# Loading the first stage's pieces of w_in from Pool's queue, and leaving adaLN's columns alone in SP's

## The chip, the cores and the metric

One core of one Trainium2 chip. The metric is the device time of one execution in microseconds; the median of three runs stands for a kernel. An execution with the hardware profiler gives the trace that is read here.

## What is computed

One conditioned layer on a sequence of 256 tokens with 2048 features, all in float32. The input is normalised, scaled and shifted by a conditioning vector (adaLN), projected to four parts of 4096 columns, gated and convolved, projected back, and added to the input through a gate; a last normalisation follows. Cut to what matters:

```python
h = rmsnorm(x, norm_g)
mod = jnp.einsum('bd,df->bf', jax.nn.silu(c), ada_w) + ada_b   # 2048 -> 3 * 2048
shift, scale, gate = jnp.split(mod, 3, axis=-1)
h = h * (1.0 + scale) + shift
proj = jnp.einsum('bsd,de->bse', h, sc_w_in)                   # 2048 -> 4 * 4096
b_gate, c_gate, v, g = jnp.split(proj, 4, axis=-1)
u = causal_depthwise_conv(c_gate * v, sc_conv_w)
y = b_gate * u * jax.nn.silu(g)
out = rmsnorm(x + gate * jnp.einsum('bse,ed->bsd', y, sc_w_out), final_g)
```

## The kernel before

**Products.** Features lie on the partitions: `hT` holds the 2048 features of the tokens as 16 blocks `k` of 128 x 256. Each float32 operand is split into a high part (float32r) and a low part (what is left), and a product takes three matmuls: high by high, weight's high by tokens' low, weight's low by tokens' high (`product`, line 495). For a piece of weights that was loaded into a tile `raw`, ACT copies the high part (`hi`, line 354) and DVE subtracts to get the low part (`lo`, line 359); then TensorE may use the piece. `raw`, `hi` and `lo` have three tiles of 1 MB each, used in turn; a piece of 512 KB takes half of one. A `raw` tile is free again when DVE has made the low parts of what is in it.

**First stage.** The first half of the columns of w_in, in 16 groups of 512 columns: four chunks `ch`, each with four quarters `q`. The products can't wait for all of adaLN, since its columns of ada_w come in during the stage: eight groups of two feature blocks. So each group of 512 columns is worked in several passes over `k` (`part`, line 520), each over the blocks that are ready by then, 56 passes in all, and the sums of a pass stay in `acc` between passes (`keep`, line 512: copied by ACT or added by DVE; line 528 seeds a bank with an earlier sum). `plan` (line 52) fixes the order of the passes and of the column loads from a table of estimated costs. The first thirteen passes take the two feature blocks that are ready at the start, 512 KB of w_in each (the first of them has its own load, line 198); the fourteenth pass takes four blocks, 1 MB, and is the first to need the second group of columns.

**adaLN's columns.** `ada_piece` (line 454) loads a piece of 512 KB in two loads (shift and scale, line 464) into one of four tiles `at`, and DVE adds it up, weighted with silu(c) (`gv`, lines 476 and 478). When a group's eight pieces are in, `ada_done` (line 480) turns the sums on TensorE (`tp_g`, line 485) and reduces them on DVE (`gs`, 486; `mod`, 324); ACT makes the high parts of two token blocks (`hT`, 328), DVE the low parts (332 and 335).

**The gate's columns.** From the last third of the stage on, `gate_piece` loads the gate's columns of ada_w (`at_g`, line 612) into the same four tiles, DVE adds them up (`gacc`, 619 and 621; two buffers, shared with `gv`), and Pool adds the sums over the partitions in seven rounds per quarter of the gate: two copies from SBUF to SBUF by DMAs that Pool issues (625, 626) and an addition (627), then one with the bias (629).

**Second and last stages.** The other half of w_in's columns in pieces of 1 MB (line 665), and then w_out (line 720), with the residual and the last normalisation.

**Queues and order.** Before the change every load of weights stands in SP's queue, in the order of the program; a load waits there until its tile is free, and all loads behind it wait too. Pool issues only the gate's copies, ACT three small loads at the start. Within each engine the framework's scheduler sets the order of the instructions from an estimated timeline, with priorities from the program (`later`, line 189). So a load that is estimated to come earlier also moves instructions on DVE, ACT and TensorE. Each engine works its instructions strictly in that order.

Of the kernel before, what the change touches and what calls it, by code (L numbers as in the profile page):

```python
# [117 lines left out]
def short_conv_layer(ctx: ExitStack, tc: tile.TileContext, x, c, norm_g, ada_w, ada_b, w_in, conv_w, w_out, final_g, out):  # L118
    nc = tc.nc
# [58 lines left out]
    @contextmanager  # L178
    def behind(last):

        traced = nc.cur_bb.bb.instructions
        n = len(traced)
        yield
        for ins in list(traced[n:]):
            if ins.engine in last:
                tc.add_manual_dep(ins, last[ins.engine], after, reason="behind")
# [111 lines left out]
    def tokens(k, part):  # L298
        return (hT[:, k] if k < KB else hT2[:, k - KB])[:, part * T : (part + 1) * T]
# [14 lines left out]
    def keep_x(j, tp):  # L314
        for i in range(CT):
            k = j * CT + i
            nc.scalar.activation(xs[j][:, i], tp[:, i], AF.Copy, scale=gT[:, k : k + 1])
# [34 lines left out]
    def split_hi(raw, n, hi=None):  # L352
        hi = hi_tile() if hi is None else hi
        nc.scalar.copy(hi[:, :n], raw[:, :n])  # L354
        return hi

    def split_lo(raw, n, hi, lo_tag="lo", lo=None):
        lo = lo_tile(lo_tag) if lo is None else lo
        last_low[0] = nc.vector.tensor_tensor(  # L359
            out=lo[:, :n], in0=raw[:, :n], in1=hi[:, :n].bitcast(F32), op=ALU.subtract  # L360
        )
        return hi, lo
# [4 lines left out]
    def places(n):  # L367

        if n <= HALF and other_half[0]:
            tiles, other_half[0] = other_half[0], None  # L370
            return [b[:, HALF:SLOT] for b in tiles]
        tiles = raw_tile("raw_s"), hi_tile(), lo_tile()
        other_half[0] = tiles if n <= HALF else None
        return tiles
# [76 lines left out]
    acc = {}  # L451
# [49 lines left out]
    def chunk_products(bank, hi, lo, o0, k, k0, k1, seed=False, late=False):  # L501


        begins = k == k0 and not seed
        terms = [(m, i) for i in (0, 2, 1) for m in range(CT)] if late else [(m, i) for m in range(CT) for i in range(3)]
        for m, i in terms:
            o = slice(o0 + m * P, o0 + (m + 1) * P)
            product(bank[:, m, :], hi[:, o], lo[:, o], k, i, begins and i == 0, m % 2 == 0, k == k1 - 1 and (m, i) == terms[-1])
# [3 lines left out]
    def keep(ch, q, k0, bank, seed=False):  # L512
        if k0 == 0 or seed:
            if k0 == 0:
                acc[ch, q] = slot([P, CT, T], f"acc{ch}{q}")
            nc.scalar.copy(acc[ch, q], bank)  # L516
        else:
            nc.vector.tensor_tensor(out=acc[ch, q], in0=bank, in1=acc[ch, q], op=ALU.add)

    def part(ch, q, k0, k1, seed):  # L520


        col = q * E + ch * CT * P
        step = SLOT // (CT * P)
        first = k0
        bank = psum.tile([P, CT, T], F32, tag="mm", name="mm_s")
        if seed:
            nc.scalar.copy(bank, acc[ch, q])  # L528
        if pieces0:
            for k in range(NK0):  # L530
                chunk_products(bank, *pieces0[k], 0, k, k0, k1, late=True)
            pieces0.clear()
            k0 = NK0
        for s0 in range(k0, k1, step):
            sk = min(step, k1 - s0)
            n = sk * CT * P
            raw, hi, lo = places(n)
            nc.sync.dma_start(
                raw[:, :n].rearrange("p (k f) -> p k f", k=sk),
                w_in[0, s0 * P : (s0 + sk) * P, col : col + CT * P].rearrange("(k p) f -> p k f", p=P),  # L540
            )
            with behind(ended if len(acc) < 3 else {}):
                split_lo(raw, n, split_hi(raw, n, hi), lo=lo)
            for i in range(sk):
                chunk_products(bank, hi, lo, i * CT * P, s0 + i, k0, k1, seed)
        if len(acc) == 1:
            with behind(ended):
                keep_x(3, tp_3)
        keep(ch, q, first, bank, seed)
# [18 lines left out]
    for kind, *step in plan():  # L568
        if kind == "ada":
            ada_piece(*step)  # L570
        else:
            ch, k1 = step[0], step[3]
            part(*step)
            if step[2] == 0 and len(acc) in LATER:
                with tc.issue_after(last_mm[0].ins), behind(ended):
                    if len(acc) == LATER[0]:
                        rows2 = rows_tile("rows2")
                        nc.sync.dma_start(rows2[:, :], conv_w.rearrange("w (k p) -> (w k) p", p=P))
                    else:
                        turn(rows2, 0, 96, cw)  # L580
            whole[ch] += k1 == KT
            if k1 == KT and whole[ch] == 4:
                mixed(ch)
# [354 lines left out]
```

## Time and profile before

| | us |
|---|---|
| median of 3 runs | 904.29 (903.64 to 904.36) |
| the profiled execution | 904.01 |
| its span, first to last instruction | 902.2 |
| TensorE busy (matmuls) | 887.1, 98% of the span |
| DVE, ACT, Pool busy | 676.2, 484.5, 88.0 |
| moved by DMA | 235.01 MB, 260 GB/s on the mean |
| of it from SP's queue and from Pool's | 226.56 MB and 7.34 MB |
| granted TensorE clock | 0.998 |

The profile page gives each engine's busy time, 40 slices of the span with a digit for the busy share in tenths, and the chain of work that ended last, followed back from the end. Further views of the trace list instructions in order of time (start, duration, engine, line, output <- inputs, and in brackets the idle time before with what ended it), who waited for whom, and the busy time of each engine in a stretch. In a row of the latter stand, after the stretch and its length, busy time and number of instructions of PE (matmuls), PEld (weight loads), DVE, ACT and POOL, then the granted clock, the DMA share and GB/s. "SPq" is the issuing of a DMA by SP; how long it takes to land is told apart.

### The profile page before, as it was taken

What the parts mean: (1) busy time and instruction counts of PE and PEld (TensorE: products, weight loads), DVE (VectorE), ACT (ScalarE), POOL (GpSimd) and SP (SyncE); (2) the same over time, 40 slices, a digit from 0 to 9 for tenths busy, and PEclk for the clock granted to TensorE, in tenths of its full rate; (3) what the DMA queues carried; (4) which work ended last, traced back from release to release, by engine and by line L of the source; (5) the groups of instructions that cost most, each with busy time, mean ns of one, the idle gap of its engine ahead of it and who ended that gap; (6) DMA issues with size and microseconds to landing.
All of it is one profiled execution on the core that took longest, in us unless ns stands there. A gap on an engine that the chain in (4) does not pass through costs nothing.

```text
span 902.2 us, 16405 instructions
## 1 busy us (share of the span) xinstructions
PE 887.1 (98%) x6997; PEld 850.1 (94%) x6997; DVE 676.2 (75%) x665; ACT 484.5 (54%) x429; POOL 88.0 (10%) x95
## 2 busy tenths in 40 slices
PE   7999999999999999999999999999999999999996
PEld 4899999999999999999999999999999988888885
DVE  5889989888888866765966677565555578879896
ACT  6767866665548766644433434444434445444443
POOL 0000000000000034024224203420000000000000
PEclk9999999999999999999999999999999999999999
DMA  9999999999998587688887788776666476674662
GB/s 309 367 369 369 362 313 353 351 370 354 350 328 289 162 277 245 194 257 243 282 242 241 249 283 259 232 221 199 198 188 188 141 288 224 191 275 132 197 231 94
DMA packets 159595, 235.01 MB, mean 260 GB/s; under 512 B 6805, under 2 KB 105285, under 8 KB 159137
## 3 DMA queue, kind: packets, MB, share of 16 engines
q1 hardware_dynamic: 156384, 226.56, 76.9%
q0 software_dynamic: 3008, 7.34, 2.9%
q8 instruction: 55, 0.90, 0.4%
q14 instruction: 20, 0.16, 0.0%
q10 hardware_dynamic: 128, 0.04, 0.0%
HBM read 224.49 MB, written 2.10 MB: 251 GB/s over the span
## 4 chain that ended last, share of the span: by engine, by line
PE 92%; DMA 4%; ACT 1%; SPq 1%; DVE 1%; issue 1%; ACTq 0%
PE mm_b L495 39%; PE mm_s L495 36%; PE mm_w L731 7%; PE mm_o L731 6%; PE mm L731 4%; DMA at<-in_ada_w_dram 2%; DMA raw_s<-in_sc_w_in_dram 1%; SPq L231 1%; ACT hi L354 1%; DMA raw_o<-in_sc_w_out_dram 1%; DMA x<-in_x_dram 1%; PE tp_g L485 0%; ACT mm_s L528 0%; ACT acc L516 0%; DVE lo L762 0%
## 5 line engine op out<-in xcount | busy, mean ns | idle before, releaser
L495 PE MATMUL mm_s<-hT,hi 128*128 128x256 f32 x2048 | 350.2, 277 | 1.7 <-ACT hT L328 1.0
L495 PE MATMUL mm_b<-hT,hi 128*128 128x256 f32 x2048 | 348.2, 276 | 0.0
L495 PEld LDWEIGHTS mm_s<-hT,hi 128*128 128x128 f32 x2048 | 308.4, 188 | 2.3 <-ACT hT L328 1.2
L495 PEld LDWEIGHTS mm_b<-hT,hi 128*128 128x128 f32 x2048 | 308.4, 188 | 0.0
L495 PE MATMUL mm_b<-hT,lo 128*128 128x256 f32 x1024 | 282.7, 276 | 0.0
L495 PE MATMUL mm_s<-hT,lo 128*128 128x256 f32 x1024 | 282.0, 277 | 0.1
L359 DVE TENSOR_TENSOR lo<-raw,hi 128x2048 fp32r<-128x2048 f32 (+1 forms) x66 | 151.9, 2302 | 99.6 <-ACT hi L354 99.4
L354 ACT CAST hi<-raw 128x2048 fp32r<-128x2048 f32 (+1 forms) x66 | 123.7, 1874 | 191.3 <-PE mm_b L495 152.4
L495 PEld LDWEIGHTS mm_b<-hT,lo 128*128 128x128 f32 x1024 | 192.3, 188 | 0.0
L495 PEld LDWEIGHTS mm_s<-hT,lo 128*128 128x128 f32 x1024 | 191.7, 188 | 0.3 <-DVE lo L359 0.3
L359 DVE TENSOR_TENSOR lo<-raw_s,hi 128x2048 fp32r<-128x2048 f32 (+1 forms) x80 | 149.8, 1877 | 40.5 <-ACT hi L354 39.9
L354 ACT CAST hi<-raw_s 128x2048 fp32r<-128x2048 f32 (+1 forms) x80 | 124.0, 1557 | 57.2 <-PE mm_s L495 51.2
L478 DVE SCALAR_TENSOR_TENSOR gv<-at,silu_c,gv 128x512 f32<-128x512 f32 x105 | 78.7, 749 | 3.6 <-DMA at<-in_ada_w_dram 1.9
L516 ACT COPY acc<-mm_s 128x1024 f32<-128x1024 f32 x54 | 54.7, 1014 | 42.1 <-PE mm_s L495 42.0
L359 DVE TENSOR_TENSOR lo<-raw_o,hi 128x2048 fp32r<-128x2048 f32 x22 | 50.4, 2291 | 23.4 <-ACT hi L354 23.4
L354 ACT CAST hi<-raw_o 128x2048 fp32r<-128x2048 f32 x22 | 42.0, 1908 | 46.2 <-PE mm_w L731 12.0
L627 POOL TENSOR_TENSOR gacc<-gacc,z 128x512 f32<-128x512 f32 x28 | 48.3, 1726 | 109.0 <-DMA z<-gacc 109.0
L731 PE MATMUL mm_w<-hi,y 128*128 128x512 f32 x184 | 58.8, 389 | 0.0
L731 PE MATMUL mm_o<-hi,y 128*128 128x512 f32 x176 | 55.3, 389 | 0.0
L621 DVE SCALAR_TENSOR_TENSOR gacc<-at_g,silu_c,gacc 128x512 f32<-128x512 f32 x60 | 46.9, 782 | 6.0 <-DMA at_g<-in_ada_w_dram 4.8
L625 POOL DMA_DIRECT2D z<-gacc x28 | 15.7, 560 | 348.7 <-DVE acc L562 284.7
L731 PEld LDWEIGHTS mm_w<-hi,y 128*128 128x128 f32 x184 | 34.5, 188 | 7.1
(153 smaller groups left out, 685.9 us busy)
## 6 DMA issues: line engine op xcount, KB each, us to landing
raw<-in_sc_w_in_dram SPq DMA_DIRECT2D x64, 1024.0 KB, 5.9
raw_s<-in_sc_w_in_dram SPq DMA_DIRECT2D x47, 1024.0 KB, 7.8
raw_o<-in_sc_w_out_dram SPq DMA_DIRECT2D x32, 1024.0 KB, 5.2
at<-in_ada_w_dram SPq DMA_DIRECT2D x114, 256.0 KB, 8.0
raw_s<-in_sc_w_in_dram SPq DMA_DIRECT2D x33, 512.0 KB, 7.1
at_g<-in_ada_w_dram SPq DMA_DIRECT2D x32, 512.0 KB, 7.9
at<-in_ada_w_dram SPq DMA_DIRECT2D x6, 512.0 KB, 9.4
x<-in_x_dram SPq DMA_DIRECT2D x4, 512.0 KB, 6.2
```

The costliest lines, as they stand in the source:

```text
L231: nc.sync.dma_start(at[:, :, s, :], adas[:, j : j + kk, s, 0 : NK0 * P])
L354: nc.scalar.copy(hi[:, :n], raw[:, :n])
L359: last_low[0] = nc.vector.tensor_tensor(out=lo[:, :n], in0=raw[:, :n], in1=hi[:, :n].bitcast(F32), op=ALU.subtract)
L478: nc.vector.scalar_tensor_tensor(out=gv, in0=at4[:, i], scalar=c_k, in1=gv, op0=ALU.mult, op1=ALU.add)
L495: mm = last_mm[0] = nc.tensor.matmul(dst, w, h[k], start=begins and left, stop=ends, skip_group_check=True)
L516: nc.scalar.copy(acc[ch, q], bank)
L621: nc.vector.scalar_tensor_tensor(out=ga, in0=at3[:, i, :], scalar=s, in1=ga, op0=ALU.mult, op1=ALU.add)
L625: nc.gpsimd.dma_start(turned[0 : P - away], ga[away:P])
L627: nc.gpsimd.tensor_tensor(out=ga, in0=ga, in1=turned, op=ALU.add)
L731: nc.tensor.matmul(dst, y[a], b, start=opens and i == 0, stop=ends and i == 2, skip_group_check=True)
```

## The change

In `part`, pieces of w_in go to Pool's queue once five groups of columns have been begun. `acc` gets an entry at the end of a group's first pass, so `len(acc) < 5` holds for the first five passes. The first has its weights from line 198; the second to the fifth load one piece each. So of the 80 loads of line 538, the first four stay with SP and the other 76 are issued by Pool.

```diff
             sk = min(step, k1 - s0)
             n = sk * CT * P
             raw, hi, lo = places(n)
-            nc.sync.dma_start(
+            queue = nc.sync if len(acc) < 5 else nc.gpsimd
+            queue.dma_start(
                 raw[:, :n].rearrange("p (k f) -> p k f", k=sk),
                 w_in[0, s0 * P : (s0 + sk) * P, col : col + CT * P].rearrange("(k p) f -> p k f", p=P),
             )
```

From line 538 on, line numbers of the changed kernel are one higher. On SP, from the fourth piece on, the rows before are these (`raw_s` is a piece of w_in, 128x2x512 being 512 KB and 128x4x512 1 MB; `at` is half a piece of adaLN's columns):

```order
L538 DMA raw_s<-in_sc_w_in_dram 128x2x512
L464 DMA at<-in_ada_w_dram 128x2x256 x4
L578 DMA rows_621<-in_sc_conv_w_dram 96x128
L538 DMA raw_s<-in_sc_w_in_dram 128x2x512 x4
L464 DMA at<-in_ada_w_dram 128x2x256 x4
L538 DMA raw_s<-in_sc_w_in_dram 128x2x512 x2
L464 DMA at<-in_ada_w_dram 128x2x256 x4
```

In the changed kernel the same place of SP reads:

```order
L539 DMA raw_s<-in_sc_w_in_dram 128x2x512
L464 DMA at<-in_ada_w_dram 128x2x256 x4
L579 DMA rows_621<-in_sc_conv_w_dram 96x128
L464 DMA at<-in_ada_w_dram 128x2x256 x104
L613 DMA at_g<-in_ada_w_dram 128x2x512 x20
L666 DMA raw<-in_sc_w_in_dram 128x8x256 x6
```

All of adaLN's remaining columns and the first 20 loads of the gate's now follow each other, held only by their own four tiles. The pieces stand on Pool, behind its one instruction for the tokens of the start and ahead of the gate's copies:

```order
L433 TENSOR_TENSOR hT<-xs_169,hT 128x256
L539 DMA raw_s<-in_sc_w_in_dram 128x2x512 x8
L539 DMA raw_s<-in_sc_w_in_dram 128x4x512 x3
L539 DMA raw_s<-in_sc_w_in_dram 128x2x512 x5
L539 DMA raw_s<-in_sc_w_in_dram 128x4x512 x6
```

DVE up to the ninth piece, before. The row of four low parts is that of the fifth to eighth pieces:

```order
L359 TENSOR_TENSOR lo<-raw_s,hi 128x1024
L478 SCALAR_TENSOR_TENSOR gv<-at,silu_c,gv 128x512 x4
L359 TENSOR_TENSOR lo<-raw_s,hi 128x1024 x4
L478 SCALAR_TENSOR_TENSOR gv<-at,silu_c,gv 128x512 x4
L359 TENSOR_TENSOR lo<-raw_s,hi 128x1024 x2
```

And in the changed kernel:

```order
L359 TENSOR_TENSOR lo<-raw_s,hi 128x1024
L478 SCALAR_TENSOR_TENSOR gv<-at,silu_c,gv 128x512 x4
L359 TENSOR_TENSOR lo<-raw_s,hi 128x1024 x2
L478 SCALAR_TENSOR_TENSOR gv<-at,silu_c,gv 128x512
L359 TENSOR_TENSOR lo<-raw_s,hi 128x1024
L478 SCALAR_TENSOR_TENSOR gv<-at,silu_c,gv 128x512 x2
```

Four sums of columns still stand ahead of the fifth piece's low part; behind it, sums are spread between the low parts, earlier than before. DVE about the thirteenth piece (the first `lo` of 128x2048), before, from the low parts of the eleventh and twelfth on:

```order
L359 TENSOR_TENSOR lo<-raw_s,hi 128x1024 x2
L486 TENSOR_REDUCE gs<-tp_g 128x4
L324 TENSOR_TENSOR mod<-gs,vec 128x2x2
L476 TENSOR_SCALAR gv<-at,silu_c 128x512
L478 SCALAR_TENSOR_TENSOR gv<-at,silu_c,gv 128x512
L359 TENSOR_TENSOR lo<-raw_s,hi 128x2048
L478 SCALAR_TENSOR_TENSOR gv<-at,silu_c,gv 128x512
L332 TENSOR_SCALAR xs_169<-xs_169,mod 128x256 x2
L478 SCALAR_TENSOR_TENSOR gv<-at,silu_c,gv 128x512
L335 TENSOR_TENSOR hT<-xs_169,hT 128x256 x2
```

In the changed kernel, from the low part of the twelfth piece on:

```order
L359 TENSOR_TENSOR lo<-raw_s,hi 128x1024
L478 SCALAR_TENSOR_TENSOR gv<-at,silu_c,gv 128x512
L486 TENSOR_REDUCE gs<-tp_g 128x4
L324 TENSOR_TENSOR mod<-gs,vec 128x2x2
L332 TENSOR_SCALAR xs_169<-xs_169,mod 128x256
L335 TENSOR_TENSOR hT<-xs_169,hT 128x256
L332 TENSOR_SCALAR xs_169<-xs_169,mod 128x256
L478 SCALAR_TENSOR_TENSOR gv<-at,silu_c,gv 128x512
L335 TENSOR_TENSOR hT<-xs_169,hT 128x256
L478 SCALAR_TENSOR_TENSOR gv<-at,silu_c,gv 128x512
L359 TENSOR_TENSOR lo<-raw_s,hi 128x2048
```

The two token blocks' low parts have moved ahead of the thirteenth piece's low part, and so have two sums of columns. On ACT the two casts of the same token blocks (line 328) stand behind that piece's high part before and ahead of it in the changed kernel.

## The prediction

> **What bounds the kernel now.** I read the page first, then busy time by stretch, then who waits for whom on TensorE, then SP, DVE and ACT in order of time where TensorE is least covered. The head, the slices and the chain:
>
> ```profile
> span 902.2 us, 16405 instructions
> PE 887.1 (98%) x6997; PEld 850.1 (94%) x6997; DVE 676.2 (75%) x665; ACT 484.5 (54%) x429; POOL 88.0 (10%) x95
> PE   7999999999999999999999999999999999999996
> DMA  9999999999998587688887788776666476674662
> PE 92%; DMA 4%; ACT 1%; SPq 1%; DVE 1%; issue 1%; ACTq 0%
> ```
>
> TensorE is busy 887.1 of 902.2 us and is 92% of the chain, so whatever delays it in the first stage stays in the total: the stages behind it have no idle time to give back. The DMA engines stand at 9 in the first twelve slices (270 us): there TensorE and the DMA engines are both full. Busy time by stretch says how full:
>
> ```profile
> 30.00:40.00 10.00, 9.36 (x84) 9.16 (x82) 8.19 (x11) 7.40 (x10) 0.00 (x0) 1.00 1.07 367
> 40.00:50.00 10.00, 10.00 (x88) 10.00 (x89) 8.96 (x10) 7.71 (x8) 0.00 (x0) 1.00 1.07 361
> 60.00:70.00 10.00, 10.00 (x91) 10.00 (x90) 9.93 (x14) 6.66 (x7) 0.00 (x0) 1.00 1.07 370
> 90.00:100.00 10.00, 9.91 (x87) 9.72 (x87) 9.75 (x13) 9.97 (x11) 0.00 (x0) 1.00 1.07 364
> 150.00:200.00 50.00, 50.00 (x443) 50.00 (x442) 43.88 (x50) 31.57 (x27) 0.00 (x0) 1.00 1.04 354
> ```
>
> A full 10 us holds 91 matmuls, 0.11 us each. 84, 88 and 87 are a loss of 7 + 3 + 4 matmuls, **1.5 us**: all that a better order of loads could win between 30 and 100 us. DMA runs at about 367 GB/s there, DVE up to 9.93 of 10.
>
> **The change, part by part.** It adds and drops no instruction: 76 loads of w_in leave SP's queue for Pool's, and the scheduler, which sees other arrival times, sets DVE's, ACT's and TensorE's rows in another order. I count pieces (loads of line 538) from one. The first four stay on SP.
>
> *A, the fifth piece, about 39 us.* The rows of SP, Pool, DVE, the landing of the four column loads issued from 24.91 on, and the piece of the chain that follows:
>
> ```profile
> 24.91 3.76 SPq L464 DMA_DIRECT2D at<-in_ada_w_dram  x4
> 27.72 0.96 SPq L464 DMA_DIRECT2D at<-in_ada_w_dram  x1
> 30.83 3.18 SPq L538 DMA_DIRECT2D raw_s<-in_sc_w_in_dram  x4
> DMA to landing us min/median/max: 8.2/8.3/8.7
> 26.02 0.91 POOL L433 TENSOR_TENSOR hT<-xs,hT 128x256 fp32r<-128x256 f32 x1 [24.71 <-ACT xs L429]
> 25.63 0.69 DVE L359 TENSOR_TENSOR lo<-raw,hi 128x512 fp32r<-128x512 f32 x1
> 28.45 1.22 DVE L359 TENSOR_TENSOR lo<-raw_s,hi 128x1024 fp32r<-128x1024 f32 x1
> 35.22 3.11 DVE L478 SCALAR_TENSOR_TENSOR gv<-at,silu_c,gv 128x512 f32<-128x512 f32 x4
> 38.69 2.52 DVE L359 TENSOR_TENSOR lo<-raw_s,hi 128x1024 fp32r<-128x1024 f32 x2 [0.35 <-ACT hi L354]
> 40.00 15.80 PE mm_s L495 x137
> ```
>
> Before, the fifth to eighth pieces are issued behind the four column loads. The last of these goes out at 27.72 and lands 8.3 later, at 36.0; the third of DVE's four sums needs it at 35.22 + 2 x 0.75 = 36.7, which leaves 0.7. DVE then waits 0.35 for ACT's half of the fifth piece, and its low part ends at 39.9, when TensorE goes on (40.00). So the columns may come 0.7 + 0.35 = 1.05 later free of charge; every further microsecond is TensorE's, for in the new order the same four sums still stand ahead of the fifth piece's low part.
>
> With the change Pool is free at 26.02 + 0.91 = 26.9, and the buffer of the fifth and sixth pieces at 25.63 + 0.69 = 26.3: both go out at about 27.0 and 27.6, 3.8 earlier than now and ahead of the last column load. The seventh and eighth need the buffer freed at 28.45 + 1.22 = 29.7 and go out then. Each is 0.52 MB, 1.43 us at 367 GB/s. DMA being full, what they take is taken from the columns and the fourth piece. Ends: nothing taken, and the 0.35 wait gone too (-0.4); all four ahead (4 x 1.43 - 1.05 = 4.65). I take two ahead and half of the other two, (2 + 1) x 1.43 - 1.05 = **3.2**: the pair at 27 is older than the last column load, the pair at 29.7 younger.
>
> No stretch of this trace has two filled queues side by side, so how they share is the open cost. The Trainium skill, "DMA: Bandwidth & Descriptors", section "Queues, rings and completion order", says that each DMA engine takes turns between queue rows packet by packet. By that, four pieces of 2.1 MB against a backlog of some 8 us would all get ahead, and the sum below would be 909.9 instead of 908.4.
>
> *B, the thirteenth piece, about 62 us.* It is the first of 1 MB, and its pass is the first with new column blocks:
>
> ```profile
> 55.67 1.23 DVE L359 TENSOR_TENSOR lo<-raw_s,hi 128x1024 fp32r<-128x1024 f32 x1 [1.30 <-ACT hi L354]
> 57.53 0.16 DVE L324 TENSOR_TENSOR mod<-gs,vec 128x4 f32<-128x4 f32 x1
> 59.72 2.29 DVE L359 TENSOR_TENSOR lo<-raw_s,hi 128x2048 fp32r<-128x2048 f32 x1 [0.80 <-ACT hi L354]
> 62.59 0.73 DVE L332 TENSOR_SCALAR xs<-xs,mod 128x256 f32<-128x256 f32 x2
> 63.90 0.75 DVE L335 TENSOR_TENSOR hT<-xs,hT 128x256 fp32r<-128x256 f32 x2
> 59.59 1.09 ACT L328 ACTIVATE hT<-xs,mod 128x256 fp32r<-128x256 f32 x2
> 62.31 1.02 ACT L516 COPY acc<-mm_s 128x1024 f32<-128x1024 f32 x1 [0.73 <-PE mm_s L495]
> ```
>
> Now its low part runs from 59.72 to 62.01, and TensorE ends the pass before at about 62.25 (ACT's copy at 62.31 waited for it): 0.25 to spare. In the new order one more sum stands ahead of gs (+0.75; the other one fits in the 1.30 wait), and between mod and the low part stand both token blocks and two sums: 0.55 until ACT's first cast, 0.38 + 0.37 + 0.38 for the rest of the tokens, 2 x 0.75, together 3.2 where 59.72 - 57.69 = 2.03 passed before. ACT's casts go ahead of its half of the piece too. Later by 0.75 + 1.15 = 1.9, less 0.25: **1.65** (0 if the stall of A let DVE get ahead, 1.9 at most).
>
> *C, given back.* A TensorE that is late finds the pieces of 90 to 100 us ready: up to 4 x 0.11 = **-0.45** (or 0).
>
> *D, Pool's issue.* SP's issue takes about 0.4. For Pool the trace has only the copies of the gate's sums, 64 to 127 rows of 2 KB; below them Pool's additions:
>
> ```profile
> L625 POOL DMA_DIRECT2D z<-gacc x28: 532/557/698, 311.6 to 593.1; - x28
> L627 POOL TENSOR_TENSOR gacc<-gacc,z x28: 1280/1298/3946, 314.8 to 596.3; 128x512 f32<-128x512 f32 x28
> ```
>
> A 1 MB piece is 512 rows. Proportional to rows (110 on the mean): 2.6 us; no dependence: 0.56. Between 64 and 127 rows it hardly moves (532 to 698), so I take 0.8. A 1 MB piece feeds TensorE for 48 x 0.11 = 5.3 us, so Pool keeps up at either end; 0.4 us of extra latency disappears behind the columns that come early. At 2.6 us each piece would be 2.2 late (a rival below).
>
> *E, the gate's sums on Pool.* They now stand behind the last piece:
>
> ```profile
> 311.61 0.70 POOL L625 DMA_DIRECT2D z<-gacc  x1 [284.68 <-DVE acc L562]
> 359.38 0.57 POOL L625 DMA_DIRECT2D z<-gacc  x1 [0.30 <-POOL gacc L627]
> 340.05 10.42 SPq L538 DMA_DIRECT2D raw_s<-in_sc_w_in_dram  x3
> L619 DVEq EVENT_SEMAPHORE  x9: 21/50/50, 424.5 to 516.9; - x9
> ```
>
> The last piece goes out at 350, so the first gate part starts 39 us later and, at its present length of about 52 (311.6 to 359.4 and the last copy and addition), ends near 404. DVE's third run of gate sums needs that buffer at 424.5: 20 us of cover. Cost nothing; without cover DVE would stand still for the rest, and TensorE behind it.
>
> **Sum:** 3.2 + 1.65 - 0.45 = 4.4 on the profiled execution's own 904.01 (span 902.2): **908.4**. The median of the three runs, 904.29, is 0.28 above that execution, well inside the bounds. What a measurement of this kernel can tell from no change is about 0.2%, 1.8 us.
>
> **Rivals.**
> - *Pool is slow.* At 2.6 us an issue, pieces are 2.2 late wherever they are used on landing: once at the thirteenth, and once more later when the early columns have used up their lead. 908.4 + 2 x 2.2 = 912.8. For it: nothing like 512 rows is in the trace. Against it: the flat 532 to 698. 0.10.
> - *DVE holds Pool up.* If Pool cannot make descriptors while DVE works, an issue waits for up to a 1 MB low part, 2.29; paid at the same two places: 908.4 + 2 x 2.3 = 913.0. For it: Pool's additions take 1280 when free and up to 3946, so something holds them. Against it: over the same 28 rounds no issue took more than 698. 0.05. The Trainium skill, "SBUF — State Buffer", section "SBUF: two separate sides", has a rule of this kind against Pool's queue: its DMAs starve while DVE runs in a two-port mode. The trace shows no issue so held.
> - *The columns keep their place.* If the engines serve loads in order of issue and the delay stays within 1.05, A is 0: 904.0 + 1.65 - 0.45 = 905.2, no measurable change. 0.17, with all smaller shares of A.
> - *Earlier pieces win.* SP's queue no longer holds a column load behind a piece that waits for its buffer, and pieces go out 3.8 earlier. If A stays within 1.05 and ACT's and DVE's order is met by earlier data, the lost matmuls (1.5) and the wait of 0.35 go: 904.0 - 1.9 = 902.1. It decides at a column delay of 1.05 us. Against it: DMA is full, and 0.52 MB alone is 1.43. 0.05.
> - *Forecast* (906.2 to 911): 0.63.
>
> **How the numbers follow.** The likeliest gives 908.4. Down, the range takes most of the second rival, to 904.9; up, the first two, to 913.0. Faster by over 0.2%: 0.05; within: 0.16 (the second rival, less what of it passes 906.1); slower: 0.79.
>
> **What would show it.** A: column loads of 27 us landing over 9.4 us after issue, DVE waiting for a DMA in the sums ahead of the fifth piece's low part, which starts near 42, and fewer than 84 matmuls from 30 to 40 or 88 from 40 to 50. B: the thirteenth piece's low part ending about 2 us behind the end of the pass before. D: Pool's issues of 0.6 to 1 us. From 110 us to the end, 443 matmuls in 50 us as before, and the last stages as long as before. It is wrong if TensorE's waits grow after 100 us (Pool too slow), or if the columns land as early as now.

## The result and the profile after

The change made the kernel slower: 912.26 us median (911.1 to 920.47) against 904.12 (903.64 to 904.36), a ratio of 1.0109 over all runs (interval 1.0065 to 1.0154) and of 1.0090 between the medians. The forecast was 908.4, 4.3 more than this 904.12; the measured step is 8.1. The direction was right and the size was not. The time also scatters now: with the repeat below, ten executions of the change lie between 911.1 and 920.5 (their median is 913.6), while the kernel before stays between 903.3 and 906.8 in all its runs beside these. The profiled execution, 920.47, is the longest of the ten, so I read in it first what all of them have.

The page of the change, head, slices and chain, against the same lines in the prediction:

```profile
span 918.7 us, 16416 instructions
PE 894.2 (97%) x6997; PEld 856.5 (93%) x6997; DVE 679.1 (74%) x665; ACT 485.3 (53%) x429; POOL 144.6 (16%) x171
PE   7799999999999999999999989999999999999996
PE 80%; DMA 11%; DVE 5%; issue 2%; SPq 1%; ACT 1%; ACTq 0%; DVEq 0%
```

No instruction of TensorE, DVE or ACT was added (6997, 665, 429 as before). Pool has 76 more: the loads. What grew in the chain is DMA, 4% to 11%, and DVE, 1% to 5%. Who waits for whom on TensorE:

```profile
PE mm_s L495 <- DVE lo L359: 7.8, 3, 4.4
PE mm_b L495 <- DVE lo L359: 2.8, 2, 2.3
```

Both rows are new: five waits for a low part, the longest 4.4 us. To see where the time goes I compare the start of the same product (they stand in one order) in both traces. The change is 0.1 us behind at the first product, 6.7 at 49 us (time of the kernel before), 8.6 at 64 and 8.3 at 96, and 8.2 still at 257. The profiled execution then loses 3.8 more near 286 us and 4.9 more between 537 and 560 us (its own time). 904.0 + 8.3 = 912.3 is the median of these four; the last two losses are this execution's own. Late losses of some size are common, though, since the ten lie 1.3 higher on the median.

**The fifth piece.** The four column loads of SP's queue (number, ns of an issue, first and last issue), with their time from issue to landing:

```profile
L464 SPq DMA_DIRECT2D at<-in_ada_w_dram x4: 368/368/788, 25.0 to 27.8; - x4
DMA to landing us min/median/max: 12.7/13.7/13.8
```

The same of Pool's first four pieces:

```profile
L539 POOL DMA_DIRECT2D raw_s<-in_sc_w_in_dram x4: 724/734/892, 27.0 to 31.0; - x4
DMA to landing us min/median/max: 7.6/8.0/8.7
```

And DVE and TensorE in order of time:

```profile
35.50 1.23 DVE L359 TENSOR_TENSOR lo<-raw_s,hi 128x1024 fp32r<-128x1024 f32 x1 [1.15 <-ACT hi L354]
40.11 3.11 DVE L478 SCALAR_TENSOR_TENSOR gv<-at,silu_c,gv 128x512 f32<-128x512 f32 x4 [3.39 <-DMA at<-in_ada_w_dram]
43.14 2.35 DVE L359 TENSOR_TENSOR lo<-raw_s,hi 128x1024 fp32r<-128x1024 f32 x2
44.41 0.58 PE L495 MATMUL mm_s<-hT,lo 128*128 128x256 f32 x1 [4.39 <-DVE lo L359]
```

The columns took 12.7 to 13.8 us where it was 8.2 to 8.7; the pieces came in 7.6 to 8.7. DVE stood 3.39 us for a column, and the fifth piece's low part, ready to be made, stood behind the four sums: TensorE waited 4.39. The DMA queues from 32 to 36 us show how the columns lost:

```profile
DMA packets 646, 1.51 MB, mean 378 GB/s; under 512 B 51, under 2 KB 348, under 8 KB 646
q0 software_dynamic: 323, 1.19, 79.2%
q1 hardware_dynamic: 323, 0.32, 24.5%
```

q0 is Pool's queue, q1 SP's; the figures are packets, MB and the share of the DMA engines' time. The packets are one for one, 323 to 323, but a packet of Pool's carries 1.19 MB / 323 = 3.7 KB and one of SP's 1.0 KB. So Pool's queue took 79% of the bytes. Of Pool's 323 packets 291 are of 4096 bytes, two rows of a piece; of SP's 297 are of 1024 bytes, one row of a column. The Trainium skill, "DMA: Bandwidth & Descriptors", section "Queues, rings and completion order", has the engines take turns between queue rows packet by packet; these counts agree, and its case is the one that came true: all four pieces got ahead. They did so although no packet of Pool's moved before 31.0 us, 3 us after the last of the four column loads had been issued. From 31 to 38.5 us:

```profile
q0 software_dynamic: 566, 2.09, 74.2%
q1 hardware_dynamic: 737, 0.74, 30.1%
```

That is 2.1 MB, all four pieces. The size of the packets decided here, not the age of the loads.

**The clock.** Busy time by stretch after that wait (length, busy time and matmuls of TensorE, granted clock, DMA share, GB/s):

```profile
40.00:42.00 2.00, 0.03 (x1) 1.00 1.10 359
42.00:44.00 2.00, 0.00 (x0) 0.72 1.04 377
44.00:46.00 2.00, 1.58 (x7) 0.50 1.05 356
46.00:48.00 2.00, 2.00 (x12) 0.50 1.12 345
48.00:50.00 2.00, 2.00 (x12) 0.57 1.04 370
50.00:52.00 2.00, 2.00 (x19) 1.00 1.00 358
```

The granted clock fell to half during the wait, at 42.9 us, and stayed there until 49.7: 12 matmuls in 2 us instead of 19. TensorE goes on at 44.41 where it was 40.00, 4.4 late, and by 49 us it is 6.7 late. The 2.3 between them are the clock's, and no term of the forecast had them.

### The profile page after: what moved, and what is told of

It reads as the page before. It is cut to its first block, busy times and chain, and to the rows that moved or that the text cites. A ratio compares the mean times of both kernels' runs of the same rounds, so it can differ in the third digit from the quotient of the medians.

```text
span 918.7 us, 16416 instructions
## 1 busy us (share of the span) xinstructions
PE 894.2 (97%) x6997; PEld 856.5 (93%) x6997; DVE 679.1 (74%) x665; ACT 485.3 (53%) x429; POOL 144.6 (16%) x171
## 4 chain that ended last, share of the span: by engine, by line
PE 80%; DMA 11%; DVE 5%; issue 2%; SPq 1%; ACT 1%; ACTq 0%; DVEq 0%
PE mm_b L495 35%; PE mm_s L495 27%; PE mm_w L732 7%; PE mm_o L732 7%; DMA at_g<-in_ada_w_dram 6%; PE mm L732 4%; DVE lo L359 3%; DMA at<-in_ada_w_dram 2%; DMA raw_s<-in_sc_w_in_dram 2%; DVE gv L478 1%; DVE gacc L622 1%; SPq L231 1%; DMA x<-in_x_dram 1%; ACT hi L354 1%; PE tp_g L485 0%
## 5 line engine op out<-in xcount | busy, mean ns | idle before, releaser
L495 PE MATMUL mm_s<-hT,lo 128*128 128x256 f32 x1024 | 285.2, 280 | 7.9 <-DVE lo L359 7.8
L495 PEld LDWEIGHTS mm_s<-hT,lo 128*128 128x128 f32 x1024 | 193.8, 190 | 8.9 <-DVE lo L359 8.9
L539 POOL DMA_DIRECT2D raw_s<-in_sc_w_in_dram x76 | 56.3, 742 | 279.9 <-DVE lo L359 269.3
L622 DVE SCALAR_TENSOR_TENSOR gacc<-at_g,silu_c,gacc 128x512 f32<-128x512 f32 x60 | 48.3, 805 | 15.8 <-DMA at_g<-in_ada_w_dram 14.8
```

What stands on the lines that cost most here:

```text
L495: mm = last_mm[0] = nc.tensor.matmul(dst, w, h[k], start=begins and left, stop=ends, skip_group_check=True)
L539: queue.dma_start(raw[:, :n].rearrange("p (k f) -> p k f", k=sk), w_in[0, s0 * P : (s0 + sk) * P, col : col + CT * P].rearrange("(k p) f - ...
L622: nc.vector.scalar_tensor_tensor(out=ga, in0=at3[:, i, :], scalar=s, in1=ga, op0=ALU.mult, op1=ALU.add)
```

## The experiments

The question was which of three things costs: that pieces and columns stand in two queues, the order that the scheduler made of the new arrival times, or Pool. So all kernels pin the rows of DVE, ACT and TensorE to a written order, that of the kernel before ("old order") or of the change ("new order"), by dependencies that wait for nothing:

```
+    for engine, flat in zip(("DVE", "Activation", "PE"), ORDER):
...
+        for a, b in zip(row, row[1:]):
+            tc.add_manual_dep(b, a.name, after, reason="order")
```

"Lag" is the start of the same product of TensorE against the trace of before. Ratios are to the runs of before beside them (medians 904.14 to 904.33).

**Queue and order taken apart.** First the change's queue with the old order.

> The pieces from Pool's queue as in the change, but the rows of DVE, ACT and TensorE pinned to the order of the kernel before. Theory (two filled queues share the DMA engines, so the columns come late): the four column sums stand ahead of the fifth piece's low part in this order too, so A stays in full, a stall of 4.4 us plus 1.8 us at a lower granted clock; B, which is a matter of order, goes. 904.1 + 6.2 - 0.4 = 909.9, and the thirteenth piece waits less than 0.5. Rival (the new order costs it all): 904.1, no change. Rival (a load from Pool's queue is slower throughout): 911 or more, with waits after 100 us.

Measured 912.88 us (912.11 to 916.66), ratio 1.0106 (1.009 to 1.0121). The lag is 5.96 at 49 us and still 5.95 at 142 us: A is there in full and B is gone, as expected. But 909.9 was missed: the profiled execution, 914.99, loses 1.9 more between 150 and 200 us and 3.7 near 544.

Then SP's queue with the new order.

> All loads in SP's queue as before, but the rows of DVE, ACT and TensorE pinned to the order of the change. Theory: no stall at the fifth piece, since its columns land 8.3 us after issue; only B, up to 1.9 at the thirteenth piece: 905 to 906. Rival (the new order costs it all): 911 to 912.

Measured 905.44 us (904.59 to 907.12), ratio 1.0013 (1.0004 to 1.0021). One wait of 1.6 us at the thirteenth piece, lag 2.03 behind it, 1.67 at 96 us, and nothing later. So the order costs 2.0 - 0.35 = 1.6 in the profiles (1.1 between the medians) and the queue the rest.

**The clock.** Matmuls that feed nothing, in the gap of the fifth piece (new order):

```
+            if len(acc) == 5:
+                fill = psum.tile([P, 512], F32, tag="sm", name="fill", bufs=2)
+                for _ in range(5):
+                    mm = nc.tensor.matmul(fill, ident, ones[:, 0:1].to_broadcast([P, 512]), start=True, stop=True)
...
```

> The change, its rows pinned to their own order, with five more matmuls (128x512, two passes each of 0.43 us, 4.3 us in all) on TensorE in the gap ahead of the fifth piece's low part; their output is used by nothing. Theory (the idle gap lowers the granted clock, which costs 1.8 us after it): matmuls behind the gap keep the pitch of 0.11 us, 912.3 - 1.8 = 910.5. Rival (the 1.8 us has another cause, data that comes late): 912.3.

Measured 910.65 us (908.95 to 913.6), ratio 1.0075 (1.0063 to 1.0088). The lag at 49 us is 4.0 where the change has 6.7, with the low part as late as there (TensorE's product behind it starts at 44.24): the clock is worth the 2.3 and a little more. Three and one in place of five:

> The change, rows pinned to their own order, with three more matmuls (2.6 us) in place of five in the gap ahead of the fifth piece's low part; some 1.8 us of idle time are left. Theory (a gap under about 2 us leaves the clock alone: 1.9 at the thirteenth piece cost nothing behind it, 2.1 near 286 us cost 1.7): matmuls behind it at 0.11 us each. Rival (any gap counts, or the sum of the gap): 0.21 us each for some 20 matmuls or more.

> The same with one more matmul (0.86 us); some 3.6 us of idle time are left. Theory: matmuls behind the gap at 0.21 us each for some 4 us, as in the change. Rival (it is the start of the gap that matters): 0.11 us each.

One execution each, 911.64 and 914.14 us; what counts is the stretch behind the gap. First three, then one:

```profile
42.00:44.00 2.00, 0.23 (x2) 1.00 1.06 378
44.00:46.00 2.00, 1.76 (x15) 1.00 1.03 346
46.00:48.00 2.00, 2.00 (x20) 1.00 1.13 334
```

```profile
42.00:44.00 2.00, 0.00 (x0) 0.90 1.07 383
44.00:46.00 2.00, 1.59 (x7) 0.50 1.03 350
46.00:48.00 2.00, 2.00 (x12) 0.50 1.12 335
48.00:50.00 2.00, 2.00 (x11) 0.50 1.01 371
```

With 2.2 us of idle time left the clock stays (lag 4.05 at 49 us), with 3.8 it drops (lag 7.05). That 2.2 us are not safe everywhere is shown in the last section. Work that is worth nothing paid for itself.

**Is it only the place of the sums?** In the new order, the low parts of the fifth and sixth pieces were moved ahead of the four sums.

> The change with its rows pinned, except that the low parts of the fifth and sixth pieces stand ahead of the four column sums on DVE. Theory (only the place behind the late columns costs the 6.2 us; the fifth piece itself landed at 34.6, in time): the low part ends near 39.8, TensorE goes on without a wait, 912.3 - 6.2 = 906.1, up to 1 us more since the columns are used 1 us later. Rival (Pool's loads are late themselves): 911 to 912.

Measured 911.0 us (909.29 to 912.22), ratio 1.0071 (1.0059 to 1.0083): the forecast missed. The fifth piece no longer waits, but the columns come no earlier, and the seventh piece's low part stands behind them instead:

```profile
43.38 1.54 DVE L478 SCALAR_TENSOR_TENSOR gv<-at,silu_c,gv 128x512 f32<-128x512 f32 x2 [1.23 <-DMA at<-in_ada_w_dram]
46.37 0.75 DVE L478 SCALAR_TENSOR_TENSOR gv<-at,silu_c,gv 128x512 f32<-128x512 f32 x1 [1.46 <-DMA at<-in_ada_w_dram]
47.04 1.22 DVE L359 TENSOR_TENSOR lo<-raw_s,hi 128x1024 fp32r<-128x1024 f32 x1
48.31 0.58 PE L495 MATMUL mm_s<-hT,lo 128*128 128x256 f32 x1 [3.17 <-DVE lo L359]
```

The wait moved from 44.4 to 48.3 us and cost 5.8. The lateness of the columns is the cause, not one place in DVE's row.

**How much is a piece?**

> Only the fifth and sixth pieces through Pool's queue, all else in SP's, rows pinned to the order of the kernel before. Theory (each piece that is issued early takes its full 1.43 us from the columns): 2 x 1.43 - 1.05 = 1.8 of stall, too short to lower the clock if the 1.9 at the thirteenth piece is a guide, so 904.3 + 1.8 = 906.1. Rival (half of each): 0.4, 904.7. Rival (it is the use of Pool's queue, not the bytes): 4.4 and more, 909 to 910.

Measured 905.62 us (904.47 to 906.88), ratio 1.0013 (1.0005 to 1.0022). TensorE waits 1.62 at the fifth piece, the lag is 1.3 and stays, and the clock does not move. Between the two ends, nearer to the full bytes.

**The roles swapped.** Columns in Pool's queue, pieces in SP's, old order (the load in `ada_piece` with `nc.gpsimd`).

> The roles swapped: adaLN's columns go through Pool's queue, all pieces stay in SP's, and the rows of DVE, ACT and TensorE are pinned to the order of the kernel before. Theory 1 (whatever is in Pool's queue is served ahead of what is in SP's): the columns land earlier than 8.3 us after issue, the pieces later, and the fifth piece's low part is not late: 904 to 906. Theory 2 (the queues take turns, and a piece's rows of 2 KB outweigh a column's of 1 KB in whichever queue): the columns land 12 us or more after issue again, the stall of 4 us or more is there, 908 to 911.

Measured 911.72 us (910.82 to 913.26), ratio 1.0083 (1.0071 to 1.0096). Neither number was right, but the place tells: the first eight column loads have free buffers, so Pool issued them at 1.3 us, beside the loads with which the kernel begins. From 10 to 14 us:

```profile
q0 software_dynamic: 293, 0.98, 69.0%
q1 hardware_dynamic: 294, 0.48, 35.0%
```

One for one again, and again Pool's packet is the larger, 3.3 KB to 1.6, although these are columns: 238 of the 293 are of 4096 bytes, now four rows of a column each. So it isn't the piece's 2 KB rows that win, as Theory 2 had it, but the queue. TensorE starts 6.5 us late, and the fifth piece, with its columns there in time, costs nothing more (lag 6.1 behind it). Near 152 and 158 us it loses 3.1, and now pieces are the late ones; ACT's cast ahead of the first of these two waits:

```profile
148.85 1.91 ACT L354 CAST hi<-raw_s 128x2048 fp32r<-128x2048 f32 x1 [4.53 <-DMA raw_s<-in_sc_w_in_dram]
```

**Later in the first stage.**

> Pieces go through Pool's queue only from the seventeenth pass on (some 65 loads), rows pinned to the order of the kernel before. Theory (only the head of the stage costs): 904.3, within 0.7. Rival (Pool's queue costs TensorE waits later too, as near 196 and 544 us in the run with Pool's queue and the old order): 906 to 907.

Measured 907.86 us (905.11 to 916.68), ratio 1.005 (1.0026 to 1.0074). The theory was wrong: Pool's queue costs without A and B too, 3.7 us on the median, and scatters (its 65 loads began at 62.1 us). DVE in the profiled execution, where TensorE lost 2:

```profile
149.00 0.75 DVE L478 SCALAR_TENSOR_TENSOR gv<-at,silu_c,gv 128x512 f32<-128x512 f32 x1 [3.17 <-DMA at<-in_ada_w_dram]
...
151.78 2.28 DVE L359 TENSOR_TENSOR lo<-raw_s,hi 128x2048 fp32r<-128x2048 f32 x1
```

It is A in small: the columns between 128 and 151 us took up to 14.0 us to land, and the low part stands behind the sum that needs them. In the trace of before this piece's low part ended 1.7 us ahead of its product (149.65 and 151.35), so a load that comes 3 late shows. Whether Pool is slow or two queues are the trouble, the next ones tell.

**One queue, but Pool's.** Columns go with the pieces from the same pass on, old order.

> From the pass at which the change moves the pieces, adaLN's columns go through Pool's queue as well, in one row with the pieces as they stood in SP's queue before; rows of DVE, ACT and TensorE pinned to the order of the kernel before. Theory (two filled queues, not Pool, cost both the stall at the fifth piece and the scattered waits after 100 us): 904.3, within 1, columns again some 8 to 9 us from issue to landing. Rival (Pool's issue and its queue are slow): 908 or more.

Measured 908.95 us (907.13 to 910.97), ratio 1.0046 (1.0032 to 1.0059). The total missed for a reason of its own: four column loads had free buffers and went out at the start, ahead of the kernel's first loads, 3.2 us before the first product. From there on the lag grows by 0.8 to 4.0 at 49 us and is still 4.05 at 484 us. Then 2.7 near 541 us. So the next one changes queue at the ninth piece and goes back to SP for the last 18:

```
+            queue = nc.gpsimd if len(acc) >= 9 and len(loads) <= 62 else nc.sync
...
+            (nc.sync if len(columns_out) <= 8 else nc.gpsimd).dma_start(at4[:, :, s, :], ...
```

> Pieces 1 to 8 and the first eight column loads in SP's queue; from then on pieces and columns together in Pool's queue, in the order they had in SP's, until piece 62; the last 18 pieces in SP's again. Rows of DVE, ACT and TensorE pinned to the order of the kernel before. Theory (two filled queues cost it, Pool's queue as such nothing): 904.2 to 905.2, no wait of TensorE over 1 us between 40 us and the second stage, and a spread of under 3 us between executions. Rival (Pool's queue is slow or uneven): 907 or more, with waits after 100 us.

Measured 909.7 us (909.03 to 909.77), ratio 1.0057 (1.0044 to 1.007). This number missed too. It lost 5.8, all of it by 56 us, where the queues change: pieces five to eight, in SP's queue, landed 8.2 to 16.4 us after issue while Pool's loads passed them. Behind that it is the kernel before, matmul for matmul, so the pinned rows cost nothing either (before, then this one):

```profile
110.00:210.00 100.00, 100.00 (x883) 1.00 1.03 348
210.00:310.00 100.00, 100.00 (x884) 1.00 0.90 304
```

```profile
110.00:210.00 100.00, 100.00 (x883) 1.00 1.00 349
210.00:310.00 100.00, 100.00 (x884) 1.00 0.93 313
```

The lag is 5.8 at 54 us and 5.8 at 726 us, and five executions lie within 0.8 us. Pool's queue as such is here neither slow nor uneven; two filled queues are.

**The gate's sums.** In five profiles (the change, e1, e9, e10, e11) TensorE also waited near 540 us, in the rest not. e9, DVE and Pool:

```profile
522.34 0.49 DVE L620 TENSOR_SCALAR gacc<-at_g,silu_c 128x512 f32<-128x512 f32 x1 [2.90 <-DMA z<-gacc]
524.84 1.68 DVE L622 SCALAR_TENSOR_TENSOR gacc<-at_g,silu_c,gacc 128x512 f32<-128x512 f32 x1 [1.23 <-DMA at_g<-in_ada_w_dram]
526.44 3.38 DVE L359 TENSOR_TENSOR lo<-raw,hi 128x2048 fp32r<-128x2048 f32 x1
524.68 1.29 POOL L628 TENSOR_TENSOR gacc<-gacc,z 128x512 f32<-128x512 f32 x1 [8.18 <-DMA z<-gacc]
526.05 1.63 POOL L630 TENSOR_TENSOR gate<-gacc,gate 128x512 f32<-128x512 f32 x1
539.24 1.54 DVE L622 SCALAR_TENSOR_TENSOR gacc<-at_g,silu_c,gacc 128x512 f32<-128x512 f32 x2 [3.52 <-DMA at_g<-in_ada_w_dram]
```

Pool ends its third run while DVE begins the fourth. A sum takes 1.68 instead of 0.75 and a low part 3.38 instead of 2.29: 2.0 us. All five profiles show these two at this place, near 530 us, and none of the others; elsewhere such long ones stand in every profile, in that of before too, and TensorE does not wait. What TensorE mainly meets in the five is a low part some 11 us later, behind sums that waited 3.3 to 3.8 us for a gate column load, as in the last row (2.1 in e5, without a wait of TensorE). That the lost 2.0 us reach that load by freeing its tile late is argued, not shown. The Trainium skill, "SBUF — State Buffer", section "SBUF: two separate sides", has Pool and DVE share one pair of ports that one holds for a whole instruction; these rows agree: DVE lost 0.93 and 1.09 where Pool's instructions had 1.13 and 1.24 left. In the repeat of the change Pool was done in time:

> The change itself once more, its rows pinned to its own order. The profiled execution of the change took 920.5 where its others took 911 to 913; it alone had two more waits of TensorE, near 286 and 549 us. Theory (these two belong to that execution): median 912 to 913, the lag against the kernel before 8.3 from 100 us to the end, so 904.0 + 8.3. Rival (they belong to the change): waits at 286 and 549 us again.

```profile
518.43 1.30 POOL L630 TENSOR_TENSOR gate<-gacc,gate 128x512 f32<-128x512 f32 x1
526.57 0.49 DVE L620 TENSOR_SCALAR gacc<-at_g,silu_c 128x512 f32<-128x512 f32 x1 [2.55 <-DMA at_g<-in_ada_w_dram]
528.60 2.28 DVE L359 TENSOR_TENSOR lo<-raw,hi 128x2048 fp32r<-128x2048 f32 x1
```

Measured 915.3 us (912.44 to 917.83), ratio 1.012 (1.01 to 1.0139). Neither theory holds as put. The profiled execution, 912.86, has no wait at 286 or 549, but one near 185 us (lag 8.5 to 9.4); the others of this kernel are up to 5 longer. The late waits belong to the change; which of them comes is a matter of the execution.

> The change with its rows pinned, but the last 18 pieces (from about 286 us on) in SP's queue again, so that Pool is free for the gate's sums some 50 us earlier. Theory (the waits near 540 us come from Pool's third run of gate sums standing beside DVE's fourth): no wait of TensorE in the second stage, A, B and the waits before 286 us as in the change: 911 to 913.5, and the third run ends before 515. Rival (they have another cause): waits near 540 again in some executions, 913 to 915.

Measured 912.41 us (910.72 to 919.97), ratio 1.0103 (1.0073 to 1.0133). No wait in the second stage of the profiled execution, and Pool's third run ended at 521.8, 4.1 before DVE's fourth began, but not before 515. One execution of 919.97 remains, so this settles less than it was meant to.

## Why the prediction was wrong, by its steps

- **A** is the step that failed, forecast 3.2, measured 6.7. Mechanism, place and order were right: the columns land late, DVE waits in the sums ahead of the fifth piece's low part. The share was wrong: "two ahead and half of the other two". All four pieces got ahead, whatever the age of the load, and the stall of 4.4 is close to the upper end that the step itself had worked out, 4 x 1.43 - 1.05 = 4.67 (put down as 4.65). I took the middle although a rule for the upper end stood beside it. The other 2.3 are the clock's, which was nowhere in the sum.
- **B**, 1.65 forecast, 1.9 measured, behind the stall of A in the change and without it in e2: the upper end again. The stall gave DVE no lead.
- **C**, -0.45 forecast, -0.35 measured between 64 and 96 us, but not by the step's mechanism. A TensorE that is 6.0 us late in the old order (e1) gets nothing back there, one that is 2.0 us late in the new order (e2) gets 0.36. So the new order gives it, not the lateness; that the size came out was luck. A full 10 us holds 88 products, as 443 in 50 us says, not the 91 of that row, which counts those that reach over its edges; the pauses near 92.5 us are 0.36 in all.
- **D** right: 0.70 to 0.89 us an issue against 0.8, 0.75 on the median of 76; 512 rows cost 0.75 where 64 to 127 had cost 0.53 to 0.70.
- **E** wrong in where it looked. The cover was measured at DVE's third run (20 us); the late start is handed on through Pool's rounds, and what it meets is the fourth. 1.8 to 4.9 us in some executions, nothing in others.
- **Not foreseen:** "From 110 us to the end, 443 matmuls in 50 us as before". Two filled queues go on side by side for 250 us more, and a load that comes 3 us late is enough where 1.7 are to spare: 0 to 3.8 us, at another place in each execution (e8: 3.7 on the median without A and B; the 3.8 in the change's profile follow 3.87 us in which ACT waited for a piece, up to 284 us). The prediction's own sign of being wrong, waits after 100 us, came, but not from a slow Pool.

6.7 + 1.9 - 0.35 is the lag of 8.3. The rival *Pool is slow* gave 912.8, next to the result, by a mechanism that is not there: issues took 0.75, and e12 runs 54 pieces with their columns through Pool's queue, without a wait from 56 us on. That its number came close is luck. The rival *the columns keep their place* fell with the landing rows, *earlier pieces win* with it, and *DVE holds Pool up* with issues that never passed 0.89.

What stays open: why Pool's queue sends these rows in packets of 4096 bytes and SP's sends each row as one, and what sets which late wait an execution gets.

## What to carry to other kernels

Loads in one queue keep an order that the program has chosen; a second filled queue gives that order up, and what it gains for one load the other queue's loads lose in full bytes. Before moving some loads to another queue, ask which loads of the old queue are needed first and how many microseconds they have to spare, everywhere, not only at the first clash. If a queue must change, change it for all that compete, and better at a point where neither side is filled: e12 lost 5.8 us by changing where both were; a change at an empty point was not tried. No kernel here was faster than the one before. Give a wait of TensorE that comes out longer than 2 us its price in clock as well.

## What the hardware showed that was not expected

The stretches of the granted clock last multiples of 3.41 us. In the change it is at half in these three, and at full in all between them:

```profile
42.89:49.72 6.83, 5.30 (x25) 0.50 1.06 357
288.65:292.07 3.42, 3.42 (x18) 0.50 0.55 172
551.48:554.89 3.41, 3.19 (x15) 0.50 0.78 262
```

288.65 and 551.48 lie 72 and 149 times 3.413 us behind 42.89; in each of the other traces, too, all changes of the clock lie on one raster of that length, each time with another offset. What tells the falls apart is TensorE's idle time within one window of the raster. The eleven windows that end with a fall (from 20 us to the last products, in all traces) hold 2.05 us of it or more. Of the windows at full clock with a pause of over 0.8 us in them, those that no fall ends hold 1.96 at most. A fall of 3.41 us cost 1.7 to 1.8 us, one of 6.83 us 2.5 to 3.0; so the same stall costs more or less as it lies on the raster (6.7 in the change, 5.96 in e1).

- Counted by their length alone, pauses of TensorE (from one product's start to the next) between 1.80 and 1.96 us, 13 in these traces, cost at most 0.3 behind them, summed over the next 90 products against their pitch of 0.113. Of five between 2.0 and 2.6 us two cost nothing (2.24 and 2.29, with 1.86 and 1.88 in their fuller window) and three 1.6 to 1.8 (2.05, 2.10, 2.53). All seven from 2.9 us on cost 1.7 to 3.0. The Trainium skill, "TensorE: Matmul & The Clock Gate", section "Part 1: The HAM clock gate (the "warmup" mystery)", names a free-running idle window of about 3.4 us. The raster agrees; that 2.05 us of idle time in a window can cost does not fit a window that must be idle throughout, and the measurement decides.
- Two queues that are both filled were served packet for packet (323 to 323, 293 to 294), so the bytes go by the size of a packet: 3.7 to 1.0 KB, 3.3 to 1.6 KB, the larger each time on Pool's queue, whose packets are mostly of 4096 bytes whether the rows are of 2 KB or of 1 KB.
- A load with a free buffer in an idle queue is issued at the start of the program, however late it is needed: in e6 eight column loads went out from 1.3 us on and moved the first product by 6.5 us, in e9 four by 3.2.
